# A fourth load tile in the first feed-forward, and its first pair of K tiles by seven products from the fifth group on

## The chip, the cores and the metric

The kernel runs on one core of one Trainium2 chip. Its engines are TensorE (PE, matmuls), VectorE (DVE), ScalarE (ACT), GpSimd (POOL) and SyncE (SP); they run their own instruction streams and wait for each other by semaphores. DMAs are issued by SP and POOL here. The metric is the time of one execution on the device in microseconds (us), as the median of several runs.

## What is computed

One layer of a streaming encoder: 256 tokens with 2048 features, float32. The stage that matters here is the first line of the layer, a feed-forward with a gate (SwiGLU) whose hidden width is 5632:

```python
D_MODEL = 2048
SEQ = 256
D_FF = 256 * ((8 * D_MODEL // 3 + 255) // 256)

def rms_norm(x, g):
    xf = x.astype(jnp.float32)
    y = xf * lax.rsqrt(jnp.mean(xf * xf, axis=-1, keepdims=True) + EPS)
    return (y * g.astype(jnp.float32)).astype(x.dtype)

def swiglu(h, w_up, w_down):
    gate, up = jnp.split(h @ w_up, 2, axis=-1)
    return (jax.nn.silu(gate) * up) @ w_down

...
        x = x + 0.5 * swiglu(rms_norm(x, ffn1_norm[l]), ffn1_w_up[l], ffn1_w_down[l])
        h = rms_norm(x, mix_norm[l])
...
        x = x + merged @ w_out[l]
        x = x + cross_attention(rms_norm(x, xattn_norm[l]), rms_norm(mem, mem_norm[l]),
                                xattn_wq[l], xattn_wkv[l], xattn_wo[l])
        x = x + 0.5 * swiglu(rms_norm(x, ffn2_norm[l]), ffn2_w_up[l], ffn2_w_down[l])
```

Between the two feed-forwards lie the mixer (a gated linear recurrence and an RG-LRU branch, merged by gates) and a cross-attention to 256 memory tokens. They are the middle stage below.

## The kernel before

**Splitting.** Every float32 operand is split into a high part in the fast matmul format and a low part, the remainder. A product of two such operands is three matmuls: high by high, high by low, low by high (`three`, L547, L548 and L550). For weights, ACT copies `raw` to `h` (L138) and DVE subtracts to get `l` (L139).

**Tiles and groups.** The hidden width is cut into 11 groups g of 512 columns. For each group, eight weight tiles of 128x2048 are loaded, one for each pair p of K tiles: a pair of 128-row K tiles by 512 gate and 512 up columns, which is a 2x2 block of 128x512 pieces. The tokens are two tiles of 128, so a pair is a 2x2 by 2x2 block product. `PRODUCTS` says how it is formed:

- "plain" and "mixed" take eight products, 24 matmuls. "mixed" adds differences of the operand (`xd`) into the same accumulators that the fast tiles use.
- "fast" takes seven products (Strassen's form, as Winograd orders it), 21 matmuls. It needs three more weight combinations beside the tile: DVE makes `td` from `raw` (L285 1024 wide, L287 and L288 512 wide each), which is split once more into `th` (ACT, two parts of 1024) and `tl` (DVE, two parts). Only three of the four quarters of `raw` are then split (1536 wide). So a fast tile takes two tiles from the pool `h` and two from `wide`.

**Tiles with an added l.** For a "fast added" tile DVE doesn't make `l`: ACT writes -raw (L293), and a DMA from POOL adds the weights to it in place (L294), after which ACT makes `h` (L295). `adds` says which these are: g above 3 and p in 3, 4, 5, 6. Down tiles with an added l, and the mixed ones of g = 3, go by `begin_added` (L254, L255), begun one step ahead.

**Order.** `ffn_order` writes out the order of all tiles. In g = 0 all eight are plain. In g = 1 and 2 even pairs are mixed, odd ones fast. In g = 3 pairs 0 and 6 are mixed. From g = 4 on the order is 1, 3, 4, 0, 2, 5, 6, 7 with pair 0 mixed and 3 to 6 fast added. After each group's eight tiles come two or four down tiles (`wd`, 24 matmuls each) of earlier groups, and the hidden values of the group just ended are turned by eight transposes (L588). A group's accumulators are combined in `ev` by ACT and DVE (L634 to L646, L580, L581) at its end, while TensorE is in the down tiles.

**Loading and looking ahead.** `weights` keeps two prepared tiles ahead of the products. SP issues the loads into `raw`, a pool of three tiles (`raw_tile`); in the second feed-forward there are two more, `raw2`, which a counter of loads picks in turn, two out of five. The pools `h` and `l` have three tiles, `wide` three. The first eight loads stand in an order written by hand; elsewhere the scheduler of the framework lays down the order in which each engine runs its instructions, and an engine runs them in that order, waiting at the head.

**Operands.** `operand_pairs` makes the operand tiles of each pair from the transposed input: `h` and `l` of the two K tiles, `less` (two differences for "mixed", in `xd` for the pairs in `BOTH`; for pair 0 it lies in the second half of its own `h` and `l`), and later `sums` (the four combinations for "fast", in that same second half; pair 0 has none in this stage). `rest` hangs such work behind certain steps of the plan.

**The second feed-forward** has fast tiles for all eight pairs; for many of them the weight sums were made during the middle stage, by `make_ahead` (POOL loads `prep`, DVE subtracts at L200, POOL stores it).

Of the kernel before, what the change touches and what calls it, by code (L numbers as in the profile page):

```python
# [8 lines left out]
F32 = mybir.dt.float32  # L9
F32R = mybir.dt.float32r  # L10
ACT = mybir.ActivationFunctionType
ALU = mybir.AluOpType

P = 128
T = 256
# [23 lines left out]
PAD = 16  # L39


def ffn_order(every=False):

    out = [(("mixed" if p > 5 else "fast") if every else "plain", 0, p) for p in range(8)]
    down = [("down", 0, 1, c, 0) for c in range(4)]  # L50
    for g in range(1, NG):
        if every:
            out += [("fast", g, p) for p in (1, 3, 4, 0, 2, 5, 6, 7)]
        elif g < 3:
            out += [(("mixed", "fast")[p % 2], g, p) for p in (0, 1, 2, 3, 5, 4, 7, 6)]
        else:
            out += [("mixed" if p == 0 or g == 3 and p == 6 else "fast", g, p)
                    for p in ((1, 3, 0, 4, 2, 6, 5, 7) if g == 3 else (1, 3, 4, 0, 2, 5, 6, 7))]
        if g > 2 and g % 2:
            down = [("down", g - 2, 2, c, b) for c in range(4) for b in (g - 2, g - 1)]  # L60
        n = 2 if g < 3 else 4
        out, down = out + down[:n], down[n:]
    return out + [("down", NG - 2, 2, c, b) for c in range(4) for b in (NG - 2, NG - 1)]


def adds(name, e):

    return name == "ffn1" and e[0] == "fast" and e[1] > 3 and e[2] in (3, 4, 5, 6)


def sums_ready(name, e):

    made = () if e[1] < 3 else (0, 5, 7) if e[1] % 2 else (0, 3, 5, 7)
    return name == "ffn2" and e[0] == "fast" and e[2] not in made
# [3 lines left out]
def block_kernel(ctx: ExitStack, tc: tile.TileContext, xT, xin, memT, vec, gfin, bgate, lruw, wu1, wd1, win, wv,  # L78
                 wg, wab, wout, wq, wk, wvm, wo, wu2, wd2, out_):
    nc = tc.nc  # L80
    pe, dve, act, sp = nc.tensor, nc.vector, nc.scalar, nc.sync

    def pool(name, bufs, **kw):
        return ctx.enter_context(tc.tile_pool(name=name, bufs=bufs, **kw))
# [6 lines left out]
    small = pool("small", 2)  # L91
    psum = pool("psum", 8, space=bass.MemoryType.PSUM)
    kept = pool("kept", 1, space=bass.MemoryType.DRAM)
    scoped = {}

    @contextmanager
    def scope(**pools):
        with ExitStack() as inner:
            for name, bufs in pools.items():
                scoped[name] = inner.enter_context(tc.tile_pool(name=name, bufs=bufs, reuse_waits="tile"))  # L100
            yield
            for name in pools:
                del scoped[name]

    def slot(dt=F32, name="slot"):
        return slots.tile([P, 1024], dt, name=name, tag="slot")

    def t1(name="t1"):
        return scoped["tmp"].tile([P, T], F32, name=name, tag="t1")

    def bank(name="acc"):
        return psum.tile([P, 512], F32, name=name, tag="acc")
# [18 lines left out]
    x = [xt[k // 4][:, (k % 4) * T:(k % 4 + 1) * T] for k in range(KT)]  # L131
    ident = col("ident", 0, P)

    done = {}


    def split(h, l, raw):
        done["high"] = act.activation(h, raw, ACT.Copy).ins  # L138
        done["low"] = dve.tensor_tensor(out=l, in0=raw, in1=h.bitcast(F32), op=ALU.subtract).ins  # L139
# [8 lines left out]
    def plan_ffn(name, wu, wd):  # L148
        for e in orders[name]:
            src = wd[e[4], e[3]] if e[0] == "down" else wu[e[1], e[2]]  # L150
            kind = "fast" if e[0] == "fast" else "added" if e[:2] == ("mixed", 3) else "plain"
            if e[0] == "down" and 0 < e[4] < NG - 1 and e[4] % 2 == 0 and e[3] % 2:
                kind = "added"
            if adds(name, e):
                kind = "fast added"
            if sums_ready(name, e):
                kind = "ready"
                t = kept.tile([P, 2048], F32, name=f"t{e[1]}_{e[2]}")
                made_ahead.append((src, t))
                src = src, t  # L160
            plan.append(((name,) + e, src, kind))
# [4 lines left out]
    def plan_rows(name, w, g):  # L166
        plan.extend(((name, g, kq), w[g, kq], "plain") for kq in range(w.shape[1]))

    plan_ffn("ffn1", wu1, wd1)
    first_middle = len(plan)  # L170
    for hf in range(2):
# [12 lines left out]
    for name, w in (("mv", wvm), ("o", wo)):  # L184
        for g in range(4):
            plan_rows(name, w, g)
    first_second = len(plan)
    plan_ffn("ffn2", wu2, wd2)

    head, rest = [], {}  # L190
# [50 lines left out]
    loads = count()  # L241

    def raw_tile():

        if "raw2" in scoped and next(loads) % 5 > 2:
            return scoped["raw2"].tile([P, 2048], F32, name="raw2", tag="raw2")
        return rawp.tile([P, 2048], F32, name="raw", tag="raw")

    def begin_added(src):

        raw = raw_tile()
        l = lp.tile([P, 2048], F32R, name="l", tag="l")
        sp.dma_start(raw, src)
        act.activation(l, raw, ACT.Copy, scale=-1.0)  # L254
        nc.gpsimd.dma_start(l, src, accum_op=ALU.add)  # L255
        return raw, l
# [100 lines left out]
    class Operands:  # L357
# [13 lines left out]
        def add(self, src, gain=None):  # L371
            t = self.new()
            if gain is None:
                act.activation(t[:, :T], src, ACT.Copy)
                dve.tensor_tensor(out=t[:, T:], in0=src, in1=t[:, :T].bitcast(F32), op=ALU.subtract)
            else:
                act.activation(t[:, :T], src, ACT.Copy, scale=gain)
                dve.scalar_tensor_tensor(out=t[:, T:], in0=src, scalar=gain, in1=t[:, :T].bitcast(F32),
                                         op0=ALU.mult, op1=ALU.subtract)
            return t  # L380
# [10 lines left out]
    class Squares:  # L391
# [2 lines left out]

        def add(self, src):
            if self.ss is None:
                self.ss = small.tile([P, T], F32, name="ss", tag="ss", bufs=1)
                act.activation(self.ss, src, ACT.Square)
            else:
                s = t1("sq")  # L400
                act.activation(s, src, ACT.Square)
                dve.tensor_tensor(out=self.ss, in0=self.ss, in1=s, op=ALU.add)

        def rstd(self):

            acc = bank()
            pe.matmul(acc[:, :T], ones, self.ss, start=True, stop=True)
            std = t1("std")
            act.activation(std, acc[:, :T], ACT.Sqrt, bias=eps, scale=1.0 / D)
            r = small.tile([P, T], F32, name="rstd", tag="rstd", bufs=2)  # L410
            dve.reciprocal(out=r, in_=std)
            return r

# [9 lines left out]
            return r  # L423


    FFN1_POOLS = dict(wide=3, hd=1, xd=2)
    FFN2_POOLS = dict(wide=2, raw2=2, hid=1, hd=1)

    class TokenSquares:
# [29 lines left out]
    def by_feature(r):  # L459

        diag = t1("diag")
        for t in range(2):
            dve.tensor_scalar(out=diag[:, t * P:(t + 1) * P], in0=ident, scalar1=r[:, t:t + 1], scalar2=None,
                              op0=ALU.mult)
        acc = bank()
        pe.matmul(acc[:, :T], ones, diag, start=True, stop=True)
        o = small.tile([P, T], F32, name="rstd", tag="rstd", bufs=2)
        act.activation(o, acc[:, :T], ACT.Copy)
        return o

# [17 lines left out]

    BOTH = [2, 4, 6]
    xd = []

    def operand_pairs(src, gain, q, xg, out, every=False):


        for a in src:
# [8 lines left out]
            if every:  # L506
                less = None
                if q == 3:
                    if not i:
                        xd.append(slot(F32R, "xd"))  # L510
                    less = [xd[-1][:, a:a + 256] for a in (512 * i, 512 * i + 256)]
            elif 2 * q + i in BOTH:
                n = 512 * (BOTH.index(2 * q + i) % 2)
                if not n:
# [4 lines left out]
        def sums(which=((0, "less"), (0, "sums"), (1, "less"), (1, "sums"))):  # L519
            s = slot(name="xs")  # L520
            for i, ((h, l), less) in enumerate(out):
                a = [xg[:, i * 512 + j * P:][:, :P] for j in range(4)]

                def made(h, l, n, at, terms):
                    o = [s[:, at + j * P:][:, :P] for j in range(n)]
                    for j, (x, y, op) in enumerate(terms(o)):
                        dve.tensor_tensor(out=o[j], in0=x, in1=y, op=op)
                    split(h, l, s[:, at:at + n * P])

                if less and (i, "less") in which:  # L530
                    made(*less, 2, 0, lambda o: ((a[0], a[1], ALU.subtract), (a[2], a[3], ALU.subtract)))
                if (every or i or 2 * q in BOTH) and (i, "sums") in which:
                    if not every and not i and len(which) > 1:
# [139 lines left out]
    pairs1, sq1 = [], TokenSquares()  # L673
# [30 lines left out]
    def late_sums(q):  # L704
        with tc.issue_after(done["low"]):
            sums1[q](((0, "sums"),))

    for q, i in ((1, 16), (2, 17), (3, 26)):
        rest[i] = lambda q=q: late_sums(q)


    par = const.tile([P, 96], F32, name="par")
    lb, oml, c8, nc8 = (par[:, i * 8:(i + 1) * 8] for i in range(4))
# [46 lines left out]

    with scope(**FFN1_POOLS):
        ffn("ffn1", pairs1, sq1, to_mix)

    middle = ExitStack()
    middle.enter_context(scope(tmp=8, tmp2=2))
    parts = middle.enter_context(ExitStack())
    parts.enter_context(scope(scores=1, extra=2, prep=1))

    xs = xs2.tiles
# [318 lines left out]
    for m in range(KT):  # L1088
        acc = two_ahead(xs3.tiles, "q", m, 0, late)
        if m == 0:  # L1090
            rstd = by_feature(sq3.rstd_tokens())
# [50 lines left out]
    for g in range(4):  # L1142
# [4 lines left out]
        for t in range(2):  # L1147
            s = slot(F32R, "vs")
            f = scoped["tmp2"].tile([P, 512], F32, name="vf", tag="part")
# [7 lines left out]
    for h in range(HEADS):  # L1157
        for j in range(4):
            acc = bank()
            for t in range(2):  # L1160
                ps = probs[h][:, t * 512:(t + 1) * 512]
                s = vs[h, t]
# [153 lines left out]
```

## Time and profile before

| | |
|---|---|
| median of 3 runs | 2423.04 us (2422.96 to 2424.28) |
| span of the profiled execution | 2425.5 us |
| TensorE busy | 2409.3 us |
| DVE busy | 2025.6 us |
| ACT busy | 1455.0 us |
| first feed-forward | about 0 to 705 us |
| middle stage | about 705 to 1765 us |
| second feed-forward | about 1765 us to the end |

The page gives no time for the profiled execution but its span. In the lines quoted below, a window's row names the stretch in us from the span's start, its length, then busy time and instruction count of each engine, the granted clock of TensorE, the busy share of the DMA engines, and GB/s. A row of the timeline is start, duration, engine, line, operation, output and inputs, how many in a row, and in brackets the idle time just before it and what ended it. Matmuls are pipelined: one lasts about 0.39 us, but the next starts after less, so their pace is read from starts. A row of waits is who waited for whom: us in total, times, and the longest.

### The profile page before, as it was taken

How to read it: one execution, taken by the hardware profiler on the slowest of the kernel's cores; microseconds unless marked ns; L12 is line 12 of the kernel's file. 1: busy time of each engine (PE TensorE's matmuls, PEld its weight loads, DVE VectorE, ACT ScalarE, POOL GpSimd, SP SyncE). 2: the span in 40 equal slices, each digit the busy share in tenths (PEclk: the TensorE clock that was granted, in tenths of full speed). 3: DMA queues.
4: the chain of work that ended last, by engine and by line, in shares of the span. 5: the costliest groups of instructions: out<-in, count | busy, mean ns of one | idle time of the engine just before them, and what ended most of it. 6: DMA issues, size and time to landing. Idle time of an engine off the chain costs nothing.

```text
span 2425.5 us, 30763 instructions
## 1 busy us (share of the span) xinstructions
PE 2409.3 (99%) x12139; PEld 2013.6 (83%) x12139; DVE 2025.6 (84%) x2260; ACT 1455.0 (60%) x1485; POOL 102.2 (4%) x166
## 2 busy tenths in 40 slices
PE   9999999999999999999999999999999999999998
PEld 8888888888788888888888888888888788888887
DVE  7999999998876868779776788777789999999995
ACT  8567677777664454476434555445676666666664
POOL 0000000000000000000000000000000000000000
PEclk9999999999999999999999999999999999999999
DMA  7579999988858776778989889977798878787873
GB/s 294 195 229 287 272 272 270 275 269 268 266 183 323 268 289 241 294 289 323 346 313 349 310 332 354 335 272 263 264 343 308 285 266 293 273 286 276 294 273 144
DMA packets 102385, 684.31 MB, mean 282 GB/s; under 512 B 11361, under 2 KB 11617, under 8 KB 29281
## 3 DMA queue, kind: packets, MB, share of 16 engines
q1 hardware_dynamic: 78192, 518.68, 57.5%
q0 software_dynamic: 23328, 162.54, 22.4%
q8 instruction: 95, 1.56, 0.2%
q10 hardware_dynamic: 720, 1.13, 0.1%
q14 instruction: 50, 0.40, 0.0%
HBM read 619.39 MB, written 62.91 MB: 281 GB/s over the span
## 4 chain that ended last, share of the span: by engine, by line
PE 91%; DVE 3%; DMA 3%; ACT 1%; issue 1%; ACTq 0%; DVEq 0%; SPq 0%
PE acc L547 16%; PE acc L548 16%; PE acc L550 16%; PE acc L313 11%; PE acc L338 8%; PE acc L341 8%; PE acc L339 8%; PE acc L316 6%; DMA raw<-wd 2%; DVE tl L139 1%; ACT h L138 1%; DVE l L139 1%; PE acc L588 1%; PE acc L477 1%; DMA t<-prep 0%
## 5 line engine op out<-in xcount | busy, mean ns | idle before, releaser
L138 ACT ACTIVATE h<-raw 128x2048 fp32r<-128x2048 f32 (+3 forms) x578 | 870.5, 1531 | 620.2 <-PE acc L339 189.6
L139 DVE TENSOR_TENSOR l<-raw,h 128x2048 fp32r<-128x2048 f32 (+2 forms) x406 | 837.3, 2065 | 187.6 <-ACT h L138 186.1
L547 PE MATMUL acc<-h,xh 128*128 128x512 f32 x1241 | 485.2, 392 | 2.7 <-ACT h L138 2.4
L548 PE MATMUL acc<-h,xl 128*128 128x512 f32 x1241 | 483.0, 390 | 0.0
L338 PE MATMUL acc<-h,ops 128*128 128x512 f32 x832 | 326.8, 393 | 0.0
L339 PE MATMUL acc<-h,ops 128*128 128x512 f32 x832 | 324.5, 390 | 0.0
L547 PEld LDWEIGHTS acc<-h,xh 128*128 128x128 f32 x1241 | 233.3, 188 | 56.2 <-ACT h L138 8.0
L547 PE MATMUL acc<-h,hidop 128*128 128x512 f32 x704 | 276.5, 393 | 2.3 <-ACT h L138 2.2
L313 PE MATMUL acc<-ops,h 128*128 128x512 f32 x1152 | 278.2, 393 | 0.0
L548 PE MATMUL acc<-h,hidop 128*128 128x512 f32 x704 | 274.8, 390 | 0.0
L548 PEld LDWEIGHTS acc<-h,xl 128*128 128x128 f32 x1241 | 233.3, 188 | 47.5
L313 PEld LDWEIGHTS acc<-ops,h 128*128 128x128 f32 x1152 | 211.7, 188 | 41.6
L139 DVE TENSOR_TENSOR tl<-raw,h 128x1024 fp32r<-128x1024 f32 x172 | 203.7, 1220 | 14.9 <-ACT h L138 14.5
L341 PE MATMUL acc<-l,ops 128*128 128x512 f32 x832 | 205.8, 389 | 0.0
L550 PE MATMUL acc<-l,hidop 128*128 128x512 f32 x704 | 189.3, 389 | 0.0
L138 ACT ACTIVATE h<-td 128x1024 fp32r<-128x1024 f32 x126 | 131.3, 1057 | 92.9 <-PE acc L548 42.3
L341 PEld LDWEIGHTS acc<-l,ops 128*128 128x128 f32 x832 | 156.2, 188 | 32.4
L338 PEld LDWEIGHTS acc<-h,ops 128*128 128x128 f32 x832 | 156.2, 188 | 32.2
L339 PEld LDWEIGHTS acc<-h,ops 128*128 128x128 f32 x832 | 156.3, 188 | 31.5
L139 DVE TENSOR_TENSOR tl<-td,h 128x1024 fp32r<-128x1024 f32 x126 | 152.0, 1220 | 31.2 <-ACT h L138 31.0
L200 DVE TENSOR_TENSOR prep<-prep 128x512 f32<-128x512 f32 x232 | 159.7, 689 | 20.9 <-DMA prep<-wu 17.1
L550 PE MATMUL acc<-l,xh 128*128 128x512 f32 x645 | 176.4, 389 | 0.0
(242 smaller groups left out, 2739.4 us busy)
## 6 DMA issues: line engine op xcount, KB each, us to landing
raw<-wu SPq DMA_DIRECT2D x114, 1024.0 KB, 6.3
raw<-wd SPq DMA_DIRECT2D x88, 1024.0 KB, 6.3
prep<-wu POOLq DMA_DIRECT2D x58, 1024.0 KB, 7.8
t<-prep POOLq DMA_DIRECT2D x58, 1024.0 KB, 7.8
raw<-t SPq DMA_DIRECT2D x58, 1024.0 KB, 6.9
raw<-wu SPq DMA_DIRECT2D x58, 768.0 KB, 5.0
raw<-win SPq DMA_DIRECT2D x40, 1024.0 KB, 4.8
raw<-wg SPq DMA_DIRECT2D x32, 1024.0 KB, 6.1
```

The source lines that it names most:

```text
L138: done["high"] = act.activation(h, raw, ACT.Copy).ins
L139: done["low"] = dve.tensor_tensor(out=l, in0=raw, in1=h.bitcast(F32), op=ALU.subtract).ins
L200: dve.tensor_tensor(out=b[o], in0=b[x], in1=b[y], op=ALU.subtract)
L313: pe.matmul(acc, h[:, k * P:(k + 1) * P], xs[k], start=k == 0, stop=False)
L316: done["product"] = pe.matmul(acc[:, :T], l[:, k * P:(k + 1) * P], xs[k][:, :T], start=False, stop=k == KT - 1).ins
L338: pe.matmul(accs[t], x[:, t * P:][:, :P], h[j], start=first and j == 0, stop=False)
L339: pe.matmul(accs[t], x[:, T + t * P:][:, :P], h[j], start=False, stop=False)
L341: done["product"] = pe.matmul(accs[t], x[:, t * P:][:, :P], l[j], start=False, stop=last and j == 3).ins
L477: pe.transpose(acc[:, z * T + t * P:][:, :P], tile[:, t * 512 + (2 * y + z) * P:][:, :P], ident)
L547: pe.matmul(acc, ah, bh, start=start, stop=False)
L548: pe.matmul(acc, al, bh, start=False, stop=False)
L550: pe.matmul(acc, ah, bl, start=False, stop=stop)
```

## The change

- The order of each group of the first feed-forward is written out in a table, `FIRST`. For g = 0 to 3 the order and kinds are those of before. From g = 4 on pair 0 is no longer "mixed" but "fast", and stands third: 1, 3, 0, 4, 2, 5, 6, 7. `adds` reads the pairs with an added l from the table; they stay 3, 4, 5 and 6.
- A fourth tile for loads, `raw1`, takes every fourth load of the first feed-forward. The counter of loads, which ran in the second feed-forward alone, now runs in the first too.
- The three small tiles of the norms (`ss`, `rstd`) leave the pool `small` for one of their own, `norms`, that lives in the middle stage only.
- Pair 0's differences move to `xd` (`BOTH` begins with 0), and `first_sums` makes its four sums at step 33 of the plan, in g = 3: it adds `h` and `l` of the pair back together (512 wide), takes four combinations of 128, and splits them into the second half of `h` and `l`.

```diff
+FIRST = [
+    "p0 p1 p2 p3 p4 p5 p6 p7",
+    "m0 f1 m2 f3 f5 m4 f7 m6",
+    "m0 f1 m2 f3 f5 m4 f7 m6",
+    "f1 f3 M0 f4 f2 M6 f5 f7",
+    "f1 a3 f0 a4 f2 a5 a6 f7",
...
+]
+KINDS = {"p": "plain", "m": "mixed", "M": "mixed", "f": "fast", "a": "fast"}
+
+def first(g):
+    return [(KINDS[e[0]], g, int(e[1])) for e in FIRST[g].split()]
...
-        elif g < 3:
-            out += [(("mixed", "fast")[p % 2], g, p) for p in (0, 1, 2, 3, 5, 4, 7, 6)]
         else:
-            out += [("mixed" if p == 0 or g == 3 and p == 6 else "fast", g, p)
-                    for p in ((1, 3, 0, 4, 2, 6, 5, 7) if g == 3 else (1, 3, 4, 0, 2, 5, 6, 7))]
+            out += first(g)
...
 def adds(name, e):
 
-    return name == "ffn1" and e[0] == "fast" and e[1] > 3 and e[2] in (3, 4, 5, 6)
+    return name == "ffn1" and e[0] == "fast" and f"a{e[2]}" in FIRST[e[1]]
...
         if "raw2" in scoped and next(loads) % 5 > 2:
             return scoped["raw2"].tile([P, 2048], F32, name="raw2", tag="raw2")
+        if "raw1" in scoped and next(loads) % 4 == 3:
+            return scoped["raw1"].tile([P, 2048], F32, name="raw1", tag="raw1")
         return rawp.tile([P, 2048], F32, name="raw", tag="raw")
...
-                self.ss = small.tile([P, T], F32, name="ss", tag="ss", bufs=1)
+                self.ss = scoped["norms"].tile([P, T], F32, name="ss", tag="ss", bufs=1)
...
-            r = small.tile([P, T], F32, name="rstd", tag="rstd", bufs=2)
+            r = scoped["norms"].tile([P, T], F32, name="rstd", tag="rstd")
...
-    FFN1_POOLS = dict(wide=3, hd=1, xd=2)
+    FFN1_POOLS = dict(wide=3, hd=1, xd=2, raw1=1)
...
-    BOTH = [2, 4, 6]
+    BOTH = [0, 2, 4, 6]
...
+    def first_sums():
+
+        (h, l), _ = pairs1[0]
+        s = slot(name="xs")
+        a, o = ([s[:, n + j * P:][:, :P] for j in range(4)] for n in (0, 512))
+        with tc.issue_after(done["low"]):
+            dve.tensor_tensor(out=s[:, :512], in0=h[:, :512].bitcast(F32), in1=l[:, :512].bitcast(F32), op=ALU.add)
+            for j, (x, y, op) in enumerate(((a[1], a[3], ALU.add), (o[0], a[0], ALU.subtract),
+                                            (a[1], a[0], ALU.subtract), (a[2], o[1], ALU.subtract))):
+                dve.tensor_tensor(out=o[j], in0=x, in1=y, op=op)
+            split(h[:, 512:], l[:, 512:], s[:, 512:])
+
+    rest[33] = first_sums
...
-    middle.enter_context(scope(tmp=8, tmp2=2))
+    middle.enter_context(scope(tmp=8, tmp2=2, norms=2))
```

More of the change, by code (lines that the diff above doesn't have):

```diff
@@ L39 @@
 PAD = 16
+FIRST = [
[11 rows of a table added]
+]
+KINDS = {"p": "plain", "m": "mixed", "M": "mixed", "f": "fast", "a": "fast"}
+def first(g):
+    return [(KINDS[e[0]], g, int(e[1])) for e in FIRST[g].split()]
 def ffn_order(every=False):
-    out = [(("mixed" if p > 5 else "fast") if every else "plain", 0, p) for p in range(8)]
+    out = [("mixed" if p > 5 else "fast", 0, p) for p in range(8)] if every else first(0)
     down = [("down", 0, 1, c, 0) for c in range(4)]
@@ L150, in plan_ffn @@
             src = wd[e[4], e[3]] if e[0] == "down" else wu[e[1], e[2]]
-            kind = "fast" if e[0] == "fast" else "added" if e[:2] == ("mixed", 3) else "plain"
+            kind = "fast" if e[0] == "fast" else "added" if name == "ffn1" and e[0] == "mixed" and f"M{e[2]}" in FIRST[e[1]] else "plain"
             if e[0] == "down" and 0 < e[4] < NG - 1 and e[4] % 2 == 0 and e[3] % 2:
@@ L466, in by_feature @@
         pe.matmul(acc[:, :T], ones, diag, start=True, stop=True)
-        o = small.tile([P, T], F32, name="rstd", tag="rstd", bufs=2)
+        o = scoped["norms"].tile([P, T], F32, name="rstd", tag="rstd")
         act.activation(o, acc[:, :T], ACT.Copy)
```

6 rows, old and new, of the table FIRST are left out of this document.

## The prediction, made before the changed kernel was run

> **What bounds the kernel now.** I read the page first, then the windows of the stage that the change touches, then that stage's waits and its timeline. TensorE is busy nearly all the time, so only its work and its stalls can set the end.
>
> ```profile
> span 2425.5 us, 30763 instructions
> ## 1 busy us (share of the span) xinstructions
> PE 2409.3 (99%) x12139; PEld 2013.6 (83%) x12139; DVE 2025.6 (84%) x2260; ACT 1455.0 (60%) x1485; POOL 102.2 (4%) x166
> ```
>
> The profiled execution gives 2425.5 as its span and no other time; the median is 2423.04. I add differences to 2425.5 and take 2.5 off at the end.
>
> The groups g = 4 to 10 of the first feed-forward repeat one pattern: eight weight tiles, then four down tiles. The next windows each run from the same matmul of one group to that of the next. The row from 2063.00 is a group of the second feed-forward, which already has eight "fast" tiles and four down tiles. The row from 94.50 lies in g = 1 and 2.
>
> ```profile
> core 0: us, PE busy (x) PEld busy (x) DVE busy (x) ACT busy (x) POOL busy (x), PEclk, DMA share, GB/s
> ...
> 441.41:503.21 61.80, 61.75 (x276) 50.88 (x276) 56.44 (x58) 44.13 (x37) 4.37 (x5) 1.00 0.91 273
> ...
> 564.96:628.53 63.57, 61.91 (x275) 50.79 (x275) 56.32 (x58) 43.83 (x37) 4.35 (x5) 1.00 0.88 268
> 2063.00:2123.74 60.74, 60.74 (x275) 50.37 (x273) 55.53 (x53) 39.49 (x35) 0.87 (x1) 1.00 0.78 273
> 94.50:150.80 56.30, 56.30 (x254) 46.47 (x253) 56.28 (x63) 30.77 (x28) 0.00 (x0) 1.00 0.56 206
> ```
>
> A group now takes 61.80, DVE works 56.44 of it, ACT 44.13. The floor for TensorE with eight fast tiles is 60.74. From 94.50 on DVE is busy without a break and TensorE does not stop: a full DVE alone is no stall.
>
> How fast matmuls follow each other is read from two starts with 48 matmuls between them: 10.88 / 48 = 0.2267.
>
> ```profile
> 444.53 0.39 PE L547 MATMUL acc<-h,hidop 128*128 128x512 f32 x1
> ...
> 455.41 0.39 PE L547 MATMUL acc<-h,hidop 128*128 128x512 f32 x1
> ```
>
> Where a group loses time, TensorE waits for the last h that ACT makes, once at each group's end (from 256 to 629):
>
> ```profile
> PEld acc L547 <- ACT h L138: 5.5, 7, 2.1
> ```
>
> DVE's own slack in a group is these three stops, and the rows between them give its pace:
>
> ```profile
> 461.29 2.36 DVE L139 TENSOR_TENSOR tl<-td,h 128x1024 fp32r<-128x1024 f32 x2 [2.11 <-ACT h L138]
> ...
> 470.38 2.36 DVE L139 TENSOR_TENSOR tl<-td,h 128x1024 fp32r<-128x1024 f32 x2 [1.75 <-ACT h L138]
> 472.66 1.22 DVE L285 TENSOR_TENSOR td<-raw 128x1024 f32<-128x1024 f32 x1
> 473.91 0.69 DVE L287 TENSOR_TENSOR td<-raw,td 128x512 f32<-128x512 f32 x1
> 474.64 0.69 DVE L288 TENSOR_TENSOR td<-raw,td 128x512 f32<-128x512 f32 x1
> 475.25 1.22 DVE L139 TENSOR_TENSOR tl<-td,h 128x1024 fp32r<-128x1024 f32 x1
> 476.38 1.22 DVE L285 TENSOR_TENSOR td<-raw 128x1024 f32<-128x1024 f32 x1
> 477.52 1.22 DVE L139 TENSOR_TENSOR tl<-td,h 128x1024 fp32r<-128x1024 f32 x1
> 478.65 2.28 DVE L139 TENSOR_TENSOR l<-raw,h 128x2048 fp32r<-128x2048 f32 x1
> 480.86 0.68 DVE L287 TENSOR_TENSOR td<-raw,td 128x512 f32<-128x512 f32 x1
> 481.46 1.75 DVE L139 TENSOR_TENSOR l<-raw,h 128x1536 fp32r<-128x1536 f32 x1
> 483.13 0.68 DVE L288 TENSOR_TENSOR td<-raw,td 128x512 f32<-128x512 f32 x1
> ...
> 489.61 2.36 DVE L139 TENSOR_TENSOR tl<-td,h 128x1024 fp32r<-128x1024 f32 x2 [1.06 <-ACT h L138]
> ```
>
> From start to start: L285 takes 1.14 (1.25 if L287 follows at once), L287 and L288 0.60 (0.73 if the next needs it), a 1024-wide tl 1.13, l 1.67 at 1536 and 2.21 at 2048 wide. All three stops wait for h, that is for TensorE to give back one of the three h tiles.
>
> **The change, part by part.** *Seven products for pair 0, seven times.* In each group the "mixed" tile of 24 matmuls becomes a fast one of 21: 7 x 3 x 0.2267 = 4.76 off TensorE. With the group ends' stalls gone as well, a group would fall to 60.74: 1.06 for an ordinary group, 2.83 for the last (63.57), and 0.68 for g = 4, of which I count the matmuls alone: 5 x 1.06 + 2.83 + 0.68 = 8.8 at best.
>
> *What DVE gets for it.* The tile's l of 2.21 goes; L285, L287, L288, l at 1536 and two tl come: 1.14 + 0.60 + 0.60 + 1.67 + 2.26 = 6.27, with some dependent starts 6.4. So +4.1 to +4.2, and DVE's 56.44 become 60.6 of the 60.74 floor. ACT's copy of 2048 becomes one of 1536 and two of 1024; its 17.7 of free time per group cover that, and only its order matters (below). Without that cover the two extra parts would be at most DVE's like, 2.3 a group.
>
> *What the order does with a full DVE.* The three stops are 4.92, and DVE has 0.1 to 0.2 left. So it must arrive later at the first two, by about 3. It may: the row of 94.50 shows TensorE at full pace beside a full DVE, and in the changed kernel's order on TensorE the first eight matmuls of the next down tile stand ahead of the last tile's remaining ones, and second halves of tl stand behind the next tile's h. I take these stops at 0.3 a group in place of 3.86, hidden under that reordering; both ends are 0 and all of 3.86.
>
> *The wait that I expect in its place.* In an "a" tile, L293 copies l on ACT and POOL then adds the weights by DMA; TensorE needs the landed l. Today, for the third such tile:
>
> ```profile
> 483.94 0.89 POOL L294 DMA_DIRECT2D l<-wu  x1 [13.27 <-DVE td L288]
> ```
> ```profile
> l<-wu POOLq DMA_DIRECT2D x1, 768.0 KB, 10.5
> ```
> ```profile
> 495.75 0.84 PE L550 MATMUL acc<-l,xh 128*128 128x512 f32 x3
> ```
>
> Issue to use is 11.8, landing 10.5: 1.3 to spare. In the changed order ACT makes that copy behind the second half of th of the tile before it, which waits for that tile's L288. Count from the first matmul of a group's first tile (467.19 in this group). DVE starts tl of the second tile at about 2.7 (now 470.38, or 3.2; ACT no longer makes another tile's l ahead of it), ends at 4.9, and then runs l 1.67, L285, L287, L288 2.59, tl 1.13, the next L285 1.13, tl 1.13, L287 0.61, tl 1.13, L288 0.61: 14.9. Then ACT: 1.1 for h, 1.5 for the copy; POOL issues 0.4 later, at about 18.0. TensorE comes to this l after five tiles and 12 matmuls: 117 x 0.2267 = 26.5. So 8.5 is left for a landing that takes 10.5 here and, for the first such tile of this group,
>
> ```profile
> l<-wu POOLq DMA_DIRECT2D x1, 768.0 KB, 7.0
> ```
>
> Behind that instruction on TensorE stands everything else, and its down tiles and the next group wait with it. I take 9.2, between the two and nearer the same tile's: 0.7 lost in a group, which gives DVE the room to lose nothing further. Ends: 0 and 2.0.
>
> *The fourth load tile.* SP's waits for tiles are long:
>
> ```profile
> SPq L279 <- DVE td L288: 107.3, 18, 8.5
> ```
>
> but they are SP's, and TensorE waits for no load in these groups; taken at 0, bounds -1.5 to 0. The same bytes move, in the same order on SP. POOL's first load for the second feed-forward leaves g = 3 for the middle stage; taken at 0 too.
>
> *The sums of pair 0* (one addition of 512, four of 128, one split) come once, in g = 3:
>
> ```profile
> L527 DVE TENSOR_TENSOR xs<-xg 128x128 f32<-128x128 f32 x22 | 5.7, 284 | 0.0
> ...
> L139 DVE TENSOR_TENSOR xl<-xg,xh 128x512 fp32r<-128x512 f32 x8 | 5.5, 691 | 11.2 <-ACT xh L138 11.2
> ```
>
> 2 x 0.69 + 4 x 0.28 = 2.5 on a DVE with 1.6 idle from 156.00 to 193.60:
>
> ```profile
> 156.00:193.60 37.60, 37.60 (x170) 30.76 (x169) 36.00 (x36) 26.38 (x22) 1.42 (x2) 1.00 0.87 277
> ```
>
> 0.9 are uncovered; I take 0.4 for TensorE, ends 0 and 2.5. *The norms' own pool and the counter of loads* (it now starts the second feed-forward at another point of its five) move addresses, no work: 0, with 1.5 either way for what first waits they may shift.
>
> Sum: a group at 60.74 + 0.7 = 61.44 saves 0.36; seven of them 2.5 (the last keeps its extra 1.8). Less 0.4: **-2.1**. 2425.5 - 2.1 = 2423.4, on the scale of the median **2421.0**.
>
> **The rivals.** *Slower: the added l lands late.* Place: third "a" tile; price: each us of landing beyond 8.5, seven times. At 9.6 nothing is gained; from about 10.2 it is 0.2% slower; at 10.5 the loss is 2.0, a group 62.74, 7 x 0.94 + 0.4 = +7, 2430. For it: today's 10.5 with DMA at 0.91 of its share; against: the 7.0. If such pauses grow past 2, the granted clock comes in:
>
> ```profile
> 1920.41 0.50 PE L547 MATMUL acc<-h,hidop 128*128 128x512 f32 x1 [2.04 <-ACT h L138]
> ```
> ```profile
> 1920.00:1925.00 5.00, 4.59 (x13) 3.65 (x14) 4.61 (x3) 5.00 (x5) 0.00 (x0) 0.66 0.73 258
> ```
>
> After 2.04 of waiting the clock is 0.66 for 5 us, 1.7 more; seven of them would make it 2442. The Trainium skill, "TensorE: Matmul & The Clock Gate", Part 1, says that the clock falls to half after an idle window of about 3.4 us; by that rule a pause of 2 would be free and the case would stay at 2430. The trace shows the loss after 2.04, so the row decides.
>
> *Slower: DVE's stops stay.* If the first two keep their 3.86, a group is 60.6 + 3.86 = 64.5, 7 x 2.7 = +19: 2442. Against: the row of 94.50.
>
> *Faster: nothing waits.* Landing under 8.5 and DVE on time: the 8.8 less 0.4, 2414.6. For it: the floor row and 7.0.
>
> *Only the matmuls go.* Stalls stay as they are and the rest is hidden anyway: -4.8, 2418.3.
>
> **How the numbers follow.** Forecast 0.38 (its own range 2418 to 2424), late landing 0.24, stops stay 0.05, nothing waits 0.24, only the matmuls 0.09. A change of 0.2% (4.85) is about what a measurement of this kernel can tell from none. Faster than 2418.2: 0.24 + 0.04 + 0.02 = 0.30; slower than 2427.9: 0.22 + 0.05 = 0.27; within: 0.43. Range 2414.5 to 2430: it takes in the floor and a landing of 10.5, and leaves out later landings and the stops.
>
> **What would show it.** Right: groups of 61.2 to 61.7 between the same matmuls; 21 matmuls fewer; DVE busy near 60.5 in a group, its stops under 1; TensorE's stop moved from the group's end to the third "a" tile, before L550 on l, with that DMA landing after 8.5. Wrong: groups of 60.8 (nothing waits), a stop of 1.5 or more there (late landing), DVE idle 3 or more in a group (stops stay), or a difference outside g = 3 to 10, above all near 1920 in the second feed-forward.

## The result, and the profile after

The changed kernel takes 2419.54 us (median of 21 runs), the kernel before 2425.35 (21 runs beside it). The ratio is 0.9977, with a 95% interval of 0.9971 to 0.9983: about 5.6 us faster, 4.1 to 7.0 by the interval. On the scale of the 2423.04 that the prediction started from this is 2417.5. The forecast was 2421.0, the range 2414.5 to 2430.0.

The head of the page of the changed kernel:

```profile
span 2419.0 us, 30802 instructions
## 1 busy us (share of the span) xinstructions
PE 2404.2 (99%) x12118; PEld 2006.5 (83%) x12118; DVE 2051.3 (85%) x2301; ACT 1463.5 (60%) x1500; POOL 102.3 (4%) x166
```

21 matmuls are gone, DVE works 25.7 us more, and the span is 6.5 shorter. Where those lie is read from windows that begin and end with the first transpose of a group (L588 before, L607 after). First the kernel before: groups 4 to 10 together, then the first and the last of them; the columns are those explained ahead of the prediction.

```profile
213.18:648.01 434.83, 432.32 (x1926) 355.95 (x1925) 394.98 (x399) 309.15 (x253) 30.45 (x35) 1.00 0.90 272
213.18:275.45 62.27, 61.74 (x276) 50.83 (x275) 57.14 (x59) 44.12 (x37) 4.32 (x5) 1.00 0.93 279
584.37:648.01 63.64, 61.98 (x276) 50.76 (x275) 55.84 (x55) 44.27 (x37) 4.37 (x5) 1.00 0.87 262
```

The changed kernel, all seven, then the first, the fourth and the last:

```profile
213.19:641.86 428.67, 428.67 (x1905) 350.46 (x1904) 418.53 (x431) 317.57 (x267) 30.52 (x35) 1.00 0.91 274
213.19:274.41 61.22, 61.22 (x273) 50.00 (x272) 59.32 (x61) 45.32 (x39) 4.37 (x5) 1.00 0.88 261
396.88:458.15 61.27, 61.27 (x273) 50.15 (x272) 60.11 (x63) 45.21 (x39) 4.38 (x5) 1.00 0.93 281
580.62:641.86 61.24, 61.24 (x273) 50.02 (x272) 58.92 (x60) 45.75 (x39) 4.38 (x5) 1.00 0.90 274
```

The seven groups give 434.83 - 428.67 = 6.16, nearly all of the 6.5. What differs outside them nearly cancels: a gain of 2.1 in the second feed-forward and a stop longer by 1.9 in the middle (both under "Outside the first feed-forward"). The seven groups start at the same time, 213.18 and 213.19, so g = 3 with its new sums costs nothing. An ordinary group goes from 61.8 to 61.25, DVE's work in it from 56.4 to 60.1.

TensorE's waits from 250 to 623, the same seven groups as in the prediction's row of before (5.5 us in 7 stops, the longest 2.1), no longer hold a long stop:

```profile
PEld acc L569 <- DVE tl L156: 3.5, 13, 0.4
PEld acc L566 <- ACT h L155: 1.8, 8, 0.3
```

The new wait that the forecast named, for the added l of the third "a" tile, is not among them. The group's first matmul and the first use of that l on TensorE, the issue on POOL, and the landing of that one transfer:

```profile
403.22 0.39 PE L566 MATMUL acc<-h,xh 128*128 128x512 f32 x1
...
431.05 0.85 PE L569 MATMUL acc<-l,xh 128*128 128x512 f32 x3
```
```profile
421.03 0.86 POOL L313 DMA_DIRECT2D l<-wu  x1 [10.16 <-ACT l L312]
```
```profile
DMA to landing us min/median/max: 7.1/7.1/7.1
```

From issue to use there are 10.0 us and the landing takes 7.1; in the other six groups it takes 6.9 to 8.4. DVE's three stops, 4.9 in a group before, have become this, from 396.88 to 458.15 (0.7 to 1.0 in the other groups, 2.1 in the first):

```profile
DVE tl L156 <- ACT h L155: 0.7, 2, 0.4
```

The last group's extra time before came from a load. Twice in the seven groups of before ACT waits, with the h of a down tile, for that tile's load: in the first group (1.5) and in the last (2.2), the two that take longer than the others:

```profile
ACT h L138 <- DMA raw<-wd: 3.8, 2, 2.2
```

ACT's timeline before, in the last group:

```profile
625.62 1.92 ACT L138 ACTIVATE h<-raw 128x2048 fp32r<-128x2048 f32 x1 [2.25 <-DMA raw<-wd]
627.44 1.04 ACT L138 ACTIVATE h<-td 128x1024 fp32r<-128x1024 f32 x1
```

ACT stands at the head of its queue with the h of the next down tile, waiting for that tile's load; behind it is the second half of th, for which TensorE waits until 628.53 (1.66). After the change ACT finds the load there and waits for TensorE instead:

```profile
621.09 3.72 ACT L155 ACTIVATE h<-raw 128x2048 fp32r<-128x2048 f32 x2 [1.10 <-PE acc L567]
624.72 1.04 ACT L155 ACTIVATE h<-td 128x1024 fp32r<-128x1024 f32 x1
```

### The profile page after: what moved, and what is told of

Same layout as the page of the kernel before. It is cut to its first block, busy times and chain, and to the rows that moved or that the text cites. A ratio compares the mean times of both kernels' runs of the same rounds, so it can differ in the third digit from the quotient of the medians.

```text
span 2419.0 us, 30802 instructions
## 1 busy us (share of the span) xinstructions
PE 2404.2 (99%) x12118; PEld 2006.5 (83%) x12118; DVE 2051.3 (85%) x2301; ACT 1463.5 (60%) x1500; POOL 102.3 (4%) x166
## 4 chain that ended last, share of the span: by engine, by line
PE 96%; DMA 2%; DVE 1%; ACT 1%; issue 0%; SPq 0%; ACTq 0%; DVEq 0%
PE acc L566 18%; PE acc L567 18%; PE acc L569 18%; PE acc L332 11%; PE acc L357 8%; PE acc L360 8%; PE acc L358 8%; PE acc L335 6%; PE acc L607 1%; PE acc L496 1%; ACT h L155 1%; DMA t<-prep 0%; DVE l L156 0%; DMA raw<-wd 0%; PE acc L1196 0%
## 5 line engine op out<-in xcount | busy, mean ns | idle before, releaser
L566 PE MATMUL acc<-h,xh 128*128 128x512 f32 x1228 | 478.3, 392 | 0.5 <-ACT h L155 0.5
L567 PE MATMUL acc<-h,xl 128*128 128x512 f32 x1228 | 476.0, 390 | 0.0
L155 ACT ACTIVATE h<-td 128x1024 fp32r<-128x1024 f32 x140 | 146.6, 1055 | 82.5 <-DVE td L304 28.3
L569 PE MATMUL acc<-tl,xh 128*128 128x512 f32 x624 | 178.1, 392 | 0.0
L156 DVE TENSOR_TENSOR tl<-td,h 128x1024 fp32r<-128x1024 f32 x140 | 169.8, 1218 | 8.9 <-ACT h L155 8.1
```

What stands on the lines that cost most here:

```text
L566: pe.matmul(acc, ah, bh, start=start, stop=False)
L567: pe.matmul(acc, al, bh, start=False, stop=False)
L569: pe.matmul(acc, ah, bl, start=False, stop=stop)
```

## The experiments

Each kernel is the changed one with the edit shown, unless another is named. "Seven groups" is the time of groups 4 to 10 between the same transposes.

| kernel | pair 0 | load tiles | seven groups | an ordinary group | ratio to before (95%) |
|---|---|---|---|---|---|
| before | mixed, fourth | 3 | 434.83 | 61.8 | 1 |
| changed | seven products, third | 4 | 428.67 | 61.25 | 0.9977 (0.9971 to 0.9983) |
| e1_three_loads | seven, third | 3 | 445.96 | 62.7 to 66.0 | 1.0045 (1.0033 to 1.0058) |
| e2_raw1_only | mixed, fourth | 4 | 432.47 | 61.8 | 0.9992 (0.9982 to 1.0001) |
| e3_neither | mixed, fourth | 3 | 436.07 | 61.8 | 1.0010 (0.9999 to 1.0022) |
| e4_order | seven, fourth | 4 | 478.07 | 68.3 | 1.0174 (1.0161 to 1.0188) |
| e5_phase | seven, third | 4 | 428.61 | 61.2 | 0.9973 (0.9964 to 0.9983) |
| e6_a0 | seven, third, added | 4 | 430.71 | 61.2 (the fifth 61.8, the last 62.8) | 0.9990 (0.9981 to 0.9998) |
| e7_a2 | seven, third; pair 2 added | 4 | 436.01 | 61.9 to 62.8 | 1.0008 (0.9998 to 1.0018) |
| e8_f5 | seven, third; pair 5 not added | 4 | 438.84 | 62.8 | 1.0018 (1.0007 to 1.0029) |
| e9_after_again | seven, third | 4 | 428.73 | 61.25 | one run |
| e10_before_again | mixed, fourth | 3 | 434.70 | 61.8 | one run |
| e11_mixed_third | mixed, third | 4 | 433.58 | 61.93 | 0.9996 (0.9987 to 1.0005) |

### The two halves of the change, apart

**e1_three_loads** takes the fourth tile away:

```diff
-    FFN1_POOLS = dict(wide=3, hd=1, xd=2, raw1=1)
+    FFN1_POOLS = dict(wide=3, hd=1, xd=2)
```

> The changed kernel without its fourth load tile (the counter of loads then runs in the second feed-forward alone, as before). Theory A (the fourth tile is what took away the 1.83 that the last group of the first feed-forward lost before, because ACT's h of a down tile waited there for its load): groups 4 to 9 stay at 61.2 to 61.5, the last rises from 61.24 to 62.5 to 63.5, ACT's wait for that load comes back; ratio to the kernel before 0.9980 to 0.9992, that is 1 to 3 us above the changed kernel. Rival B (the seven products and their new order alone took that wait away; the tile is worth nothing, as the prediction said): all groups at 61.2 to 61.3, ratio 0.9972 to 0.9982. Rival C (with three load tiles the seven products make a group wait for loads): 62 or more in each, ratio 1.000 or more.

Rival C holds. The seven groups take 17.3 longer than with four tiles, and the kernel is slower than before. Two of its groups:

```profile
339.69:405.69 66.00, 62.58 (x273) 49.73 (x272) 60.51 (x63) 45.30 (x39) 4.36 (x5) 1.00 0.87 253
405.69:468.77 63.08, 62.05 (x273) 50.00 (x272) 60.19 (x63) 45.56 (x39) 4.37 (x5) 1.00 0.88 267
```

Its waits from 275 to 580, a stretch of the same length in both: ACT's waits for weight loads, and TensorE's for ACT:

```profile
ACT l L312 <- DMA raw<-wu: 7.8, 10, 1.7
ACT h L155 <- DMA raw<-wu: 6.7, 3, 4.3
PEld acc L566 <- ACT h L155: 15.6, 22, 2.5
```

In the changed kernel the first two rows are not there, the third is a tenth, and the only wait for a load is for down tiles:

```profile
PEld acc L566 <- ACT h L155: 1.6, 7, 0.3
ACT h L155 <- DMA raw<-wd: 3.5, 5, 0.8
```

L307 is the last reader of a fast tile's raw on DVE. The longest of these waits, from DVE through SP and ACT to TensorE:

```profile
368.32 0.69 DVE L307 TENSOR_TENSOR td<-raw,td 128x512 f32<-128x512 f32 x1
369.07 0.33 SPq L298 DMA_DIRECT2D raw<-wu  x1
380.29 1.48 ACT L155 ACTIVATE h<-raw 128x1536 fp32r<-128x1536 f32 x1 [4.26 <-DMA raw<-wu]
381.83 0.50 PE L566 MATMUL acc<-h,xh 128*128 128x512 f32 x1 [2.11 <-ACT h L155]
```

SP issues the load, that of the group's last weight tile, when DVE has freed a tile. This is 29.4 after the group's first transpose (28.4 in the next group). In the kernel before, also with three tiles, that load is issued after 23.0 (the group from 399.07), in the changed kernel after 21.3 (the group from 396.88). So with the seven products in their new place DVE frees a tile for that load 5 to 6 later in a group, and with three tiles ACT stands waiting when the load is due. With four the load is already there. No run has three tiles and only one of the two, the products or the place, so what each adds to this delay is not shown.

**e2_raw1_only** keeps the fourth tile and takes the seven products out, **e3_neither** takes both out:

```diff
-    "f1 a3 f0 a4 f2 a5 a6 f7",
+    "f1 a3 a4 m0 f2 a5 a6 f7",
...
-    rest[33] = first_sums
```

For e3_neither the edit of e1_three_loads is made as well.

> The fourth load tile (and the norms' pool and the place of pair 0's differences) without the seven products: pair 0 mixed, fourth in a group as before, no sums made in g = 3. Theory A: ordinary groups as before, 61.7 to 61.8, the last 61.6 to 62.0 in place of 63.6; ratio to the kernel before 0.9985 to 0.9995. Rival B: last group still above 63, ratio 0.9995 to 1.0005. Rival C (loads set every group): ordinary groups fall to 61.4 or less, ratio under 0.9985.

> Neither the fourth load tile nor the seven products: of the change there is left the norms' own pool and pair 0's differences in another tile. Both theories: the groups of before (61.75, the last 63 to 64), ratio 0.9995 to 1.0005. If these moved addresses matter by themselves, another ratio. Also a second look at three places outside the first feed-forward in which the two profiles differ: about 998 (before 0.94 idle, after 2.88), about 1906 (after 0.64) and about 1915 to 1925 (before 2.2 and a clock of 0.66, after 1.44 and none). If these are of the execution and not of the kernel, this profile differs from that of before there.

For e2_raw1_only theory A holds: ordinary groups are those of before, the last is like them. Its last group, and that of e3_neither:

```profile
583.80:645.59 61.79, 61.74 (x276) 50.87 (x275) 54.64 (x54) 44.53 (x37) 4.39 (x5) 1.00 0.91 273
```
```profile
583.70:649.06 65.36, 63.34 (x276) 52.01 (x275) 54.99 (x54) 44.66 (x37) 4.92 (x6) 0.97 0.91 277
```

Over the seven groups of e2_raw1_only ACT waits for no load at all. So with pair 0 mixed the fourth tile is worth 2.4 and 2.2 us against the two profiles of before, in the first of the seven groups and the last; the whole time moves too little to tell it from none (the interval of the ratio ends at 1.0001). Against e3_neither it is 3.6, but that is not the price of a load tile. The time of e3_neither is that of before within its interval, and its first group takes 61.75; its last group is longer, by another way than before. Its scheduler's order puts a load for the second feed-forward on POOL in front of the last added tile of that group, whose landing then takes 15.9 (12.2 in e2_raw1_only, without that load in front); TensorE waits for it:

```profile
606.96 0.87 POOL L212 DMA_DIRECT2D prep<-wu  x1
611.85 0.85 POOL L313 DMA_DIRECT2D l<-wu  x1 [4.02 <-ACT l L312]
```
```profile
627.80 0.50 PE L569 MATMUL acc<-l,xh 128*128 128x512 f32 x1 [2.02 <-DMA l<-wu]
```

**e11_mixed_third** keeps the order and the fourth tile, with pair 0 mixed:

```diff
-    "f1 a3 f0 a4 f2 a5 a6 f7",
+    "f1 a3 m0 a4 f2 a5 a6 f7",
...
-    rest[33] = first_sums
```

> The changed kernel with pair 0 mixed (24 matmuls, no sums in g = 3) but still third in a group: the new order and the fourth load tile without the seven products. Theory A (the order by itself gives nothing; in the changed kernel the seven products give 0.55 a group): groups of 61.7 to 61.8 as with pair 0 mixed and fourth, ratio 0.9985 to 0.9998. Rival B (the order takes the wait for h at a group's end away by itself): 61.4 to 61.5, the floor of 60.74 and three matmuls, ratio 0.998 or less. Rival C (third is a bad place for a mixed tile): 62 or more.

Its groups take 61.93, a little over theory A's and below rival C's: the order by itself loses 0.15 a group.

```profile
337.24:399.17 61.93, 61.70 (x276) 50.86 (x275) 56.80 (x57) 44.00 (x37) 4.33 (x5) 1.00 0.91 272
```

Against the changed kernel's 61.25 the seven products save 0.68 a group, which is 3 x 0.2267 = 0.68: the three matmuls, and on balance nothing else. Over the seven groups the steps add up: the fourth tile takes off 2.36 (434.83 to 432.47), the new order gives back 1.11 (to 433.58), and the seven products take off 4.91 (to 428.67).

### The place in the order, and the added l

**e4_order** puts pair 0 back to the fourth place:

```diff
-    "f1 a3 f0 a4 f2 a5 a6 f7",
+    "f1 a3 a4 f0 f2 a5 a6 f7",
```

> The changed kernel with pair 0 fourth, as before, in place of third: 1, 3, 4, 0, 2, 5, 6, 7. Theory A (DVE is nearly full and the place of the tile whose l DVE itself makes decides how its work is spread): two added tiles then stand together and four tiles of DVE's own l less so; groups of 61.3 to 62.0, ratio 0.9975 to 1.0000. Rival B (the order is nothing): 61.2 to 61.3, ratio 0.9972 to 0.9982.

It is far worse than either theory said: 68.3 a group. This is the prediction's slower rival, in a neighbouring kernel. A group, the issues of the last two added tiles, and TensorE's stop before the third one's l:

```profile
418.69:487.05 68.36, 63.64 (x273) 51.68 (x272) 60.16 (x62) 45.51 (x39) 4.38 (x5) 0.95 0.81 246
```
```profile
446.21 0.86 POOL L313 DMA_DIRECT2D l<-wu  x1 [17.69 <-ACT l L312]
447.58 0.86 POOL L313 DMA_DIRECT2D l<-wu  x1 [0.52 <-ACT l L312]
```
```profile
456.34 1.22 PE L569 MATMUL acc<-l,xh 128*128 128x512 f32 x2 [4.65 <-DMA l<-wu]
```

Two fast tiles whose l DVE makes itself, 0 and 2, now follow each other just ahead of the third added one, and its transfer is issued 456.34 - 4.65 - 446.21 = 5.5 before TensorE comes to it, where the changed kernel has 10.0. The landing takes 10.1, not 7.1. So the 2.9 to spare become a stop of 4.65. The stop also lowers the granted clock, to 0.95 over the group: TensorE is busy 63.64 in place of 61.27, which is the rest of the 7. Why the landing is longer is not shown. The next added tile's transfer starts 1.4 behind it and not 2.9, but in the kernel before, where it starts some 5 behind, the third one's landing took 8.9 to 11.7.

**e6_a0** and **e7_a2** give a fifth tile an added l, **e8_f5** takes one of the four away:

```diff
-    "f1 a3 f0 a4 f2 a5 a6 f7",
+    "f1 a3 a0 a4 f2 a5 a6 f7",
```
```diff
-    "f1 a3 f0 a4 f2 a5 a6 f7",
+    "f1 a3 f0 a4 a2 a5 a6 f7",
```
```diff
-    "f1 a3 f0 a4 f2 a5 a6 f7",
+    "f1 a3 f0 a4 f2 f5 a6 f7",
```

> The changed kernel with a fifth added l, that of pair 0: 1, 3, 0, 4, 2, 5, 6, 7 with 3, 0, 4, 5, 6 added. DVE then works 1.67 less in a group: 58.4 in place of 60.1. Theory A (DVE, 60.1 of 61.24, is what holds the half us above the floor of 60.74): groups of 60.75 to 60.95, ratio 0.995 to 0.997. Rival B (the added l of a tile lands late once three of them stand in a row, as with pair 0 fourth): a stop before the l of an added tile, groups of 62 to 68, ratio 1.000 or more. Rival C (neither): 61.2.

> The changed kernel with a fifth added l, that of pair 2, between the fourth and the fifth: 4, 2, 5, 6 in a row are added. DVE 58.4 in a group. Theory A as for pair 0: 60.75 to 60.95, ratio 0.995 to 0.997. Rival B (late landing): more likely here than with pair 0, since four follow each other and POOL's transfers take 7 to 10 each: groups of 62 to 68, ratio 1.000 or more.

> The changed kernel with one added l less: pair 5's l is made by DVE. DVE then has 60.1 + 1.7 = 61.8 of work in a group. Theory A (DVE is now the bound): groups of 61.8 to 62.6, TensorE's stops behind DVE's tl grow, ratio 0.9990 to 1.0015. Rival B (TensorE is still the bound and DVE has room through the interleaved order): 61.2 to 61.4, ratio 0.997 to 0.998. Rival C (as with pair 0 fourth, where the place of the added tiles decides): 64 or more.

A group of each, in this order (for e7_a2 its longest):

```profile
335.09:396.30 61.21, 61.21 (x273) 50.11 (x272) 58.57 (x62) 46.55 (x40) 5.23 (x6) 1.00 0.95 288
```
```profile
338.32:401.08 62.76, 61.03 (x273) 50.30 (x272) 58.80 (x62) 46.23 (x40) 5.23 (x6) 1.00 0.95 281
```
```profile
337.81:400.64 62.83, 62.34 (x273) 49.80 (x272) 61.54 (x64) 44.31 (x38) 3.48 (x4) 1.00 0.81 248
```

With 1.5 less on DVE a group of e6_a0 still takes 61.21, and TensorE still waits for tl (0.6 in it), so rival C: DVE's sum is not what holds the half us above the floor of 60.74. Then in its last group late landing comes in (62.84). In e7_a2 it comes in every group, as rival B has it:

```profile
374.42 0.97 PE L569 MATMUL acc<-l,xh 128*128 128x512 f32 x3 [1.73 <-DMA l<-wu]
```

In e8_f5 DVE's 61.5 do show: 62.8 a group, a little above theory A's 62.6, with TensorE's stops before h and not before tl. So the changed kernel stands in a corner. One tile's l more for DVE costs 1.6 a group; one tile's l more by DMA costs nothing to 1.6, and the DMA engines are then busy 0.95 of their time.

### Outside the first feed-forward

**e5_phase** gives the first feed-forward its own counter of loads, so that the second starts where it did before:

```diff
-    loads = count()
+    loads, loads1 = count(), count()
...
-        if "raw1" in scoped and next(loads) % 4 == 3:
+        if "raw1" in scoped and next(loads1) % 4 == 3:
```

> The changed kernel with a counter of its own for the loads of the first feed-forward, so that the second starts at the point of its five load tiles at which it started before. Theory A (the point matters little): first feed-forward as in the changed kernel (groups of 61.2), the second as spread as in the runs so far (its first losses between 1900 and 1990 were 7.5 in the kernel before and 4 to 6 in the others), ratio to the kernel before 0.9970 to 0.9985. Rival B (the new starting point is what took about 2 off the second feed-forward near 1915): that loss comes back with a wait of 2 or more for a down tile's load and a clock under 0.7 behind it, ratio 0.9980 to 0.9995.

Theory A: the time is that of the changed kernel, and g = 2 of the second feed-forward does not get its loss back (rows below).

**e9_after_again** and **e10_before_again** are the two kernels unedited, for a second profile of each.

> The changed kernel once more, unedited, for a second profile. Theory A: the first feed-forward is the kernel's (groups of 61.2 again, its end within 0.5 of 697.5), and the two places outside it (the stop of 2.88 near 994 in the middle, the losses of 1906 to 1920 in the second feed-forward) are the execution's: either differs by more than 0.5 from the first profile. Rival B: both come again within 0.3, so they belong to the changed kernel.

> The kernel before once more, unedited. Theory A: ordinary groups 61.75, the last again 63 or more, ACT's h of a down tile waiting there for its load; the loss of some 7 us between 1900 and 1990 differs from the first profile by more than 1. Rival B: the last group falls to 62 or less, so its extra time was of one execution and not the kernel's.

The first feed-forward repeats: the seven groups of the changed kernel take 428.73 (first profile 428.67), those of before 434.70 (434.83). Within the seven, before moves: its first group takes 63.25 in place of 62.27, its last 62.43 in place of 63.64, both times with ACT waiting for the down tile's load in the last. Neither theory of e10_before_again had that; the sum stays.

The stop in the middle, near 1000, is the execution's. TensorE waits there for DVE 0.94 in the first profile of before and 2.74 in the second, 2.88 in the first profile of the changed kernel. In the second profile of the changed kernel 0.4 of waiting is left there, so theory A of e9_after_again holds for this place; near 1915 the changed kernel's two profiles agree (pauses of 1.27 and 1.21), as rival B has it.

Group 2 of the second feed-forward, in both profiles of before, both of the changed kernel, and e5_phase:

```profile
1884.82:1939.86 55.04, 52.44 (x224) 41.88 (x223) 49.60 (x47) 34.69 (x30) 0.88 (x1) 0.97 0.79 279
```
```profile
1885.99:1940.98 54.99, 52.46 (x224) 41.88 (x223) 50.39 (x47) 34.79 (x30) 0.88 (x1) 0.97 0.80 281
```
```profile
1880.55:1933.48 52.93, 51.16 (x224) 40.74 (x223) 49.05 (x46) 34.50 (x30) 0.89 (x1) 1.00 0.79 279
```
```profile
1877.93:1930.44 52.51, 50.75 (x224) 40.82 (x223) 48.97 (x46) 34.60 (x30) 0.89 (x1) 1.00 0.79 280
```
```profile
1879.11:1931.42 52.31, 50.83 (x224) 40.81 (x223) 48.97 (x46) 34.62 (x30) 0.89 (x1) 1.00 0.79 282
```

Before loses some 2 us more here, twice, the changed kernel not. e5_phase shows that the counter's starting point isn't the cause; e3_neither, with the old point and three tiles, stands between (54.0). Nor does either half of the change explain it alone: e1_three_loads, with three tiles, takes 53.1 and e2_raw1_only, with pair 0 mixed, 53.3. Of the 2 us some 1.7 are the granted clock, which in before falls after a pause of about 2 near 1920; the changed kernel pauses 1.2 to 1.3 there and keeps its clock. Why its pause is shorter stays open. The result does not hang on it: the two kernels' times differ by 5.6, and the seven groups alone give 6.0 to 6.2.

## Why the prediction was right, and where it was not

The time lies in the range and below the forecast: forecast -2.1, measured -5.6 (4.1 to 7.0). The likeliest case, no change beyond 0.2%, did not come out clearly: 0.23%, with an interval from 0.17 to 0.29. Nearest is the rival "only the matmuls go" (-4.8), to which the prediction gave 0.09.

That the range held is in part luck. It was worked out with the fourth load tile at nothing, and without that tile the same seven products come out 11 us slower than before (e1_three_loads), which on the prediction's scale is 2434 and outside the range. A group's 61.25 lies close to the forecast's 61.44, but by other stops than the one that was forecast.

Of the signs that the prediction gave for being right, the groups of 61.2 to 61.7, the 21 matmuls and the short stops of DVE came; TensorE's stop before the third added l did not. One of its signs for being wrong came as well: a difference near 1920 in the second feed-forward, 2.1 and 2.5 in the two pairs of profiles.

- *Seven products: 4.76.* Right. e11_mixed_third against the changed kernel gives 0.68 a group, 433.58 - 428.67 = 4.9 over seven.
- *DVE: +4.1 to +4.2, to 60.6 in a group.* A little high: 60.1 in the group from 396.88, and +3.4 a group over the seven. That DVE's first two stops would go was right (4.9 in a group to 0.7), and so the rival "stops stay" fell.
- *The new wait for the third added tile: 0.7 a group.* This step failed, in one term. The issue was placed at 18.0 after the group's first matmul; it came at 421.03 - 403.22 = 17.8. The room was taken as 8.5 and was 10.0, since TensorE came to that l 27.8 after the same matmul and not 26.5, with some 121 matmuls ahead of it and not 117. The landing was taken as 9.2 and was 6.9 to 8.4, at the fast end of the two rows. The half us that a group still loses above 60.74 goes by the waits to a few stops of up to 0.4 before tl and h, not to this. The mechanism is real: e4_order, with 5.5 of room and 10.1 of landing, loses 7 us a group to it.
- *"The last keeps its extra 1.8."* Failed, and was the largest miss: the last group went from 63.64 to 61.24 and the first from 62.27 to 61.22, 3.45 together (in the second profiles 62.43 and 63.25 to 61.24 and 61.21, 3.2), where 0.7 had been counted.
- *The fourth load tile at 0, since TensorE waits for no load in these groups.* Failed at its reason. TensorE's own wait named ACT; ACT, one step back, waited for the load. With pair 0 mixed the tile is worth 2.2 to 2.4 over the seven groups (434.70 and 434.83 to 432.47). With the seven products in their new place it is worth 17.3 (e1_three_loads): DVE frees the load tiles later, and three are then too few. No rival of the prediction had that, because it costed the parts one by one.
- *The sums of pair 0: 0.4.* They cost nothing: both kernels reach the first transpose of g = 3 at 213.2.
- *The clock.* The prediction let the row decide in which the clock fell after a pause of 2.04. The runs bear that row out (pauses of 1.98 and 2.02 were followed by 0.70 and 0.67 over the next 5 us), though pauses of 2.11 and 2.63 cost nothing (last section). The Trainium skill, "TensorE: Matmul & The Clock Gate", Part 1, also says that the window of about 3.4 us runs freely. That would fit this irregularity, which no run here traces to it; a fall after 2 us does not fit the length.

## What to carry to other kernels

Follow a wait back until it ends at something that the change touches: "TensorE waits for ACT" was "ACT waits for a load" one step further, and an extra buffer was the cure. Cost the parts of a change together: here the seven products in their new place, alone, lose 11 us, the fourth tile alone wins some 2, and both win 5.6, because work added to an engine that frees buffers makes the buffers scarcer. Where a tile is prepared through a copy and a DMA, its place in the order can be worth more than the work saved: here one exchange of neighbours cost 7 us a group, where seven products save 0.68.

## What the runs showed of the hardware

An added transfer of 768 KB lands after 6.7 to 12.6 us in the seven groups of the changed kernel. A group's third takes 6.9 to 8.4, its fourth, issued 2.7 to 2.9 behind the third, 11.6 to 12.6. In e3_neither one took 15.9, with a transfer of 1 MB issued 4.9 ahead of it on POOL. The distance to the next transfer alone does not set it: the third takes 8.9 to 11.7 in the kernel before, where the fourth is issued some 5 behind.

The granted clock does not follow the length of a pause alone. After 1.98 (e10_before_again) and 2.02 (e3_neither) it was 0.70 and 0.67 over the next 5 us:

```profile
1921.52 0.50 PE L547 MATMUL acc<-h,hidop 128*128 128x512 f32 x1 [1.98 <-ACT h L138]
```
```profile
1921.00:1926.00 5.00, 4.48 (x13) 3.55 (x14) 4.50 (x3) 5.00 (x5) 0.00 (x0) 0.70 0.71 256
```
```profile
627.80:633.00 5.20, 5.20 (x16) 4.12 (x17) 2.99 (x3) 4.13 (x3) 0.00 (x0) 0.67 0.78 326
```

After the pause of 2.11 in e1_three_loads, whose row stands above, it stayed at 1.00:

```profile
381.83:386.83 5.00, 4.78 (x20) 3.62 (x21) 5.00 (x5) 3.72 (x4) 0.00 (x0) 1.00 0.42 175
```

It also stayed at 1.00 after 2.63 (e3_neither, 1921.09) and after 2.74 and 2.88 (the stops near 1000 in e10_before_again and the changed kernel), and was 0.66 after 3.28 (e6_a0, 996.06) and 0.53 after 4.65 (e4_order, 456.34). A pause of two to three us may cost 1.7 more or nothing; the runs do not show what decides.
